# A two-layer hybrid decoder step: buffers for the S5 state tables, order of the first attention scores, and input projections by halves

## The chip, the cores and the metric

The kernel runs on one core of a Trainium2 chip. The metric is the device time of the program in microseconds, taken as the median of several executions. One further execution was recorded by the hardware profiler, and all trace times below are from it.

## The reference, cut to what matters

One inference step of two layers over 576 tokens: a prompt of 512 and 8 sequences of 8 new tokens each. Each layer has a token mixer with three branches on the same input and a channel mixer (dense SwiGLU in layer 0, top-2 of 8 experts in layer 1). Everything is fp32.

```python
def token_mixer(h, l, p, s5_re0, s5_im0, conv0, ssd0, past):
    gates, u, q, k, v, fg, z, xbc, dt_raw = jnp.split(h @ p['w_in'][l], _in_split_points(), axis=-1)
    gates = jax.nn.sigmoid(gates.reshape(bsz, seq, N_BRANCH, D_MODEL) + p['b_gate'][l])
    y_s5, s5_re, s5_im = s5_branch(u, s5_re0, s5_im0, ...)      # 32 groups of 16 channels, 64 complex states
    logf = jax.nn.log_sigmoid(fg + p['b_fgate'][l])
    y_fox = fox_prompt(q, k, v, logf) or fox_sample(...)        # 8 heads of 64, softmax with forget decay
    y_ssd, conv_new, ssd_new = ssd_branch(z, xbc, dt_raw, ...)  # y * silu(z), then an RMS norm
    merged = (gates[:, :, 0] * (y_s5 @ p['w_branch_s5'][l])
              + gates[:, :, 1] * (y_fox @ p['w_branch_fox'][l])
              + gates[:, :, 2] * (y_ssd @ p['w_branch_ssd'][l]))
    return merged @ p['w_o'][l], (k, v, logf, s5_re, s5_im, conv_new, ssd_new)

def run_trunk(x, p, ...):
    for l in range(2):
        x = layer_norm(ALPHA * x + token_mixer(x, l, ...), ln1_g[l], ln1_b[l])
        f = swiglu(x, ...) if l == 0 else moe_swiglu(x, ...)
        x = layer_norm(ALPHA * x + f, ln2_g[l], ln2_b[l])
```

The model width is 1024, each branch is 512 wide. The outputs are the tokens and all new states.

## The kernel before, in words

**Layout.** The input x lies transposed in SBUF, channels on 128 partitions and the 576 tokens along the free axis, as a high and a low part (`xh`, `xl`) whose sum is the fp32 value. A weight block of 128 output columns is loaded by SP (`wload`, L266, 512 KB), split into `wh` on ACT (L98) and `wl` on DVE (L107), and multiplied by `mm3` (L290 to L297): for each half of the tokens (288) and each of eight blocks of the contraction three matmuls, so 24 matmuls a half block and 48 a block. `colblocks` (L301) does this for several blocks in a row; with `by_half` it goes through all blocks for the first half of the tokens and then loads and splits the weights again for the second half.

**Order.** SP issues its DMAs in program order. The instructions of all other engines are ordered ahead of time by a planner, which simulates the engines and gives precedence by program order. `tc.issue_after(ins)` puts the instructions of its block behind `ins` on that instruction's engine. Tiles come from pools with a fixed number of buffers for each tag; a new tile waits until the tile that had the buffer before is no longer read. In the mixer's phases tag A has 7 buffers, T has 3, and K and Q have 1 each. PSUM has two buffers for `mm`, `px` and `pf` and one for `pa` and `p5`.

**Start.** Five tiles of x are loaded and transposed (`x_tr`), the first two blocks of the S5 projection u are loaded early, and `u_proj(0)` (L709) runs with hooks that put the transposes of x, the parameter DMAs (`params_dma`, 13 small ones, L693 and L695) and the steps of the S5 preparation (`s5_steps`, 14 small DMAs, L342 to L360) between its half blocks.

**Mixer** (L727). In both layers the forget gates (`fd`) come first, then the convolution state; then, in layer 1, `u_proj(1)`. In layer 0 u_proj ran at the start, and eight gate blocks stand in this place. Then come the convolution and SSD, keys, queries, values and attention (`kqv_fox`, L803), the S5 scan and its output loop, sampled attention, filler projections (gates and z that are needed later), the S5 gated unit and its product.

**Attention.** `kqv(j)` projects the K, Q and V blocks of two heads, transposes them and stores them to DRAM through ACT's queue; the last evictions are at L830. `kqv(0)` and `kqv(1)` come before the first head. For each of 8 heads and 4 blocks of queries, `front` loads kT and qT (POOL's queue), computes the scores (L886) and the softmax on DVE and ACT, and three units later `back` transposes the probabilities and multiplies by V (L909).

**S5 output loop** (L607 to L632). For each quarter q of the groups, ACT's queue loads `tu` (eight DMAs, tag T) and `cu`, the tables that carry the state (two DMAs, L613, tag A); eight pairs of matmuls for each of two halves add the products (L621 with tu, L622 with cu) into one PSUM tile (`p5`), which ACT evicts as `yg` before a GELU on DVE and ACT.

**Merge.** `mixer_end` (L1554) loads the attention output, calls `gate_z` (L1219), which multiplies the SSD output by the z gates and normalises it (squares on ACT summed on POOL, a matmul with ones at L1242, a square root, a reciprocal), and then `merge` (L1368): for eight column blocks the gated product of branch 1 (`front`), and, three blocks later, that of branch 2 (`back`), which alone needs the result of gate_z.

**End.** `combine` normalises five tiles of tokens and applies scale and shift with 1024 columns, 768 on DVE and 256 on POOL (L1913 to L1931).

Of the kernel before, what the change touches and what calls it, by code (L numbers as in the profile page):

```python
# [19 lines left out]
P = 128  # L20
D = 1024
# [13 lines left out]
NOV = -(-(576 - CAP) // CAP)  # L35
LT = (NOV + 1) * CAP
FLAG, SLAG, ZLAG = 3, 1, 1
CD_ = 768
NPRE, NPS, NPP = 5, 2, 1
LAGE = 1  # L40
NZ = (1, 1)
# [5 lines left out]
def decoder_step(ctx, tc, A, O):  # L47
# [251 lines left out]
    HS = (slice(0, HF), slice(HF, T))  # L299

    def colblocks(src, c0, ncol, kt, x, evac, by_half=False, first=()):  # L301
        first = list(first)
        for hs in (((0,), (1,)) if by_half else ((0, 1),)):
            for j in range(ncol // P):
                w = wsplit(first.pop(0) if first else wload(src, c0 + j * P, P, kt), P, kt)
                o = [MM()[:, :HF] for h in hs]
                mm3(o, w, kt, x, [HS[h] for h in hs])
                for h, o_ in zip(hs, o):
                    evac(j, h, o_)
# [198 lines left out]
    def s5_scan_and_out(l):  # L508
# [97 lines left out]
        for q in range(4):  # L606
            tus = U("T", [P, 8, P], name="tu")  # L607
            for s in range(8):
                act.dma_start(out=tus[s * 16:(s + 1) * 16],
                              in_=KZ[l][q, :, (1 + s) * 16:(1 + s) * 16 + P].rearrange("(g c) t -> c g t", c=16))  # L610
            cu = UA([P, 2, 4, 144], name="cu")
            for i in range(2):
                act.dma_start(out=cu[i * 64:i * 64 + 64],  # L613
                              in_=CD[l][:, i, q * 4:q * 4 + 4].rearrange("(a n) g t -> n a g t", a=2))
            for a in range(2):
                tu = tus[:, a:8:2]
                pt = P5()
                pv = pt[:, :288].rearrange("p (g k) -> p g k", g=4)
                for g in range(4):
                    gp = q * 4 + g  # L620
                    pe.matmul(pv[:, g, :], lhsT=tu[:, g, :], rhs=uc[a][:, gp, :], start=True, stop=False)  # L621
                    pe.matmul(pv[:, g, :], lhsT=cu[:, a, g, 16:144], rhs=vs[a][:, gp, 0:72], start=False, stop=True)  # L622
                yv = yg[a][:, q * 4:q * 4 + 4, :]
                y2v = [wk.tile([P, HF], F32, name="ygl", tag="v288", bufs=4).rearrange("p (g k) -> p g k", g=4)
                       for i in range(2)]
                cp(yv, pv)
                mul(dve, y2v[0], yv, yv)
                dve.tensor_scalar(y2v[0], y2v[0], 0.044715, 1.0, op0=OP.mult, op1=OP.add)
                mul(dve, y2v[0], y2v[0], yv)
                act.activation(y2v[1], y2v[0], AF.Tanh, scale=math.sqrt(2.0 / math.pi))  # L630
                stt(yv, y2v[1], 1.0, yv, OP.add, OP.mult)
# [94 lines left out]

    def mixer(l):  # L727
        w_in = A["w_in"][l]
        raw = wload_fd(w_in)
        w = wsplit(raw, 16, 8)  # L730
        fd = wk.tile([16, T], F32, name="fd", tag="xp", bufs=4)
# [45 lines left out]
        cp(cs8.rearrange("p a b -> p (a b)"), pt[:, :192])  # L777
        S["cs8"] = cs8

        if l:  # L780
            u_proj(l)
        else:
            for j in range(8):
                gate_out(l, 0, j)
                if j % 2:
                    with tc.issue_after(S["mm"].ins):
                        next(s5g)
                    next(s5g, None)
# [17 lines left out]
    def kqv_fox(l, w_in):  # L806
# [60 lines left out]
        def front(hp, i, h2):  # L867
            if i == 0 and h2 == 0:
                kqv_[hp] = U("V", [P, 512], name="vt")
                pool.dma_start(out=kqv_[hp], in_=VD[l][hp])  # L870
            h = 2 * hp + h2
            if i == 0:
                kq_[h] = kT, qT = U("K", [P, 2, 512], F32R, name="kT"), U("Q", [P, 512], F32R, name="qT")
                hd = slice(h2 * 64, h2 * 64 + 64)
                for a in range(2):
                    pr_ = slice(a * 64, a * 64 + 64)
                    pool.dma_start(out=kT.bitcast(F32)[pr_], in_=KD[l][hp][hd])
                    pool.dma_start(out=qT.bitcast(F32)[pr_], in_=QD[l][hp][hd, a])
                cb_[h] = U("CB", [P, 512], name="cb")
                pool.dma_start(out=cb_[h], in_=CTD[l][h].unsqueeze(0).to_broadcast([P, 512]))  # L880
            kT, qT = kq_[h]
            n = (i + 1) * P
            qs = slice(i * P, n)
            pt = PF()
            for a in range(2):
                pe.matmul(pt[:, :n], lhsT=qT[:, qs], rhs=kT[:, a, 0:n], start=(a == 0), stop=(a == 1))  # L886
            s_ = W5("s")
            stt(s_[:, :n], pt[:, :n], ct[:, i, h:h + 1], cb_[h][:, :n], OP.add, OP.subtract)
            sub(dve, s_[:, qs], s_[:, qs], pos)
            sm = wk.tile([P, 3], F32, name="smx", bufs=4)  # L890
            dve.tensor_reduce(sm[:, 0:1], s_[:, :n], axis=AX.X, op=OP.max, negate=True)
            act.activation(s_[:, :n], s_[:, :n], AF.Exp, bias=sm[:, 0:1], accum_out=sm[:, 1:2])
            dve.reciprocal(sm[:, 2:3], sm[:, 1:2])
            dve.tensor_scalar(s_[:, :n], s_[:, :n], sm[:, 2:3], None, op0=OP.mult)
            return s_
# [449 lines left out]
            pool.dma_start(out=t[2], in_=GD[l][j])  # L1345
            act.dma_start(out=MD[l][j], in_=gated(l, 0, j, yv, t)[2])

    def merge(l, yf, ys, mhl):
        seq = [(2, j) for j in range(8)] if 1 in SPILL[l] else \
            [(1, 0), (1, 1), (1, 2)] + [x for j in range(5) for x in ((1, j + 3), (2, j))] + [(2, 5), (2, 6), (2, 7)]  # L1350
        ready = {}
# [6 lines left out]
        def front(j):  # L1358
# [6 lines left out]
            else:  # L1365
                gates(GLEAD)
                t = ready.pop((1, j))
            t = gated(l, 1, j, yf, t)  # L1368
            for h in range(2):
                add(dve, m5[:, HS[h]], m5[:, HS[h]], t[h])  # L1370
            return m5

        def back(j, m5):
            gates(GLEAD)
            t = gated(l, 2, j, ys, ready.pop((2, j)))
            for h in range(2):
                add(dve, m5[:, HS[h]], m5[:, HS[h]], t[h])
                split(mhl[0][:, j, HS[h]], mhl[1][:, j, HS[h]], m5[:, HS[h]])
# [174 lines left out]

    def mixer_end(l, out, done=None):  # L1554
        yf = load_yf(l)
        ys = gate_z(l, A["w_in"][l])
        mhl = [V2([U("M", [P, 2, T], F32R, name=f"m{q}{i}") for i in range(4)]) for q in "hl"]
        merge(l, yf, ys, mhl)
        mixer_out(l, mhl, out, done)

    with phase("mix0", **MA):
# [5 lines left out]
        for i in range(3):  # L1567
            x_tr(i)
        gather_logs(0)
        s5g = s5_steps(0)  # L1570
        u_proj(0, (((0, 0), lambda: x_tr(3)), ((1, 0), lambda: x_tr(4)), ((1, 0), lambda: params_dma(0)),
                   ((2, 0), lambda: next(s5g)), ((0, 1), lambda: params_tr(0)), ((1, 1), lambda: next(s5g)), ((3, 1), lambda: next(s5g))), uw)
        mixer(0)
    with phase("mix0b", **MB):
        mixer_end(0, to_x)
# [335 lines left out]
    def combine(yy):  # L1911
# [3 lines left out]
        for i in range(5):  # L1915
# [5 lines left out]
            act.activation(ag[:n, 2:3], ag[:n, 1:2], AF.Sqrt, scale=ALPHA ** 2, bias=eps[:n, 0:1])  # L1921
            dve.reciprocal(ag[:n, 2:3], ag[:n, 2:3])
            stt(ag[:n, 3:4], ag[:n, 0:1], -1.0, ag[:n, 2:3], OP.mult, OP.mult)
            cc = (slice(0, CD_), slice(CD_, D))
            for en, cs in ((pool, cc[1]), (dve, cc[0])):
                act.activation(xt[:n, cs], xt[:n, cs], AF.Identity, scale=ag[:n, 2:3], bias=ag[:n, 3:4])
                mul(en, xt[:n, cs], xt[:n, cs], lb_[:n, 0, cs])
                add(en, xt[:n, cs], xt[:n, cs], lb_[:n, 1, cs])
            c0, c1 = cc
            o = O[0][0, i * P:(i + 1) * P] if i < 4 else O[1].rearrange("b t d -> (b t) d")  # L1930
            sp.dma_start(out=o, in_=xt[:n])  # L1931

# [83 lines left out]
```

## Time and profile before

| what | value |
|---|---|
| median of 3 runs | 2424.92 us (2424.42 to 2428.13) |
| profiled execution, its own time | 2409.88 us |
| its span | 2408.2 us |
| PE busy | 2284.0 us (95%) |
| DVE busy | 1578.5 us (66%) |
| ACT busy | 1142.8 us (47%) |
| POOL busy | 565.6 us (23%) |
| HBM traffic over the span | 166 GB/s |

The busy shares are averages over stages. PE is the engine with the least idle time, so a stage is read by two columns: PE's busy time in it, and the clock that PE was granted. Times in a trace are counted from the span's start.

### The profile page before, as it was taken

To read this page: it belongs to the slowest core of one execution; us is meant where nothing else is said; L and a number is where in the kernel's file an instruction comes from. 1 tells how busy PE (TensorE), PEld (TensorE's weight loads), DVE (VectorE), ACT (ScalarE), POOL (GpSimd) and SP (SyncE) were. 2 spreads that over 40 slices of the span, in tenths; PEclk is the share of its full clock that TensorE was granted. 3 is DMA by queue.
4 is the path that set the end of the run, shared out by engine and by line. 5 is a ranking of instruction groups with operands and counts; after the bars stand their busy time and mean duration, and the time that the engine had idled before them with its cause. 6 is when DMAs were issued, how large, how long until landed. Compare 5 with 4: busy or idle time off the path is not lost. (4 is left out here: it accounts for less than half of the span.)

```text
span 2408.2 us, 45404 instructions
## 1 busy us (share of the span) xinstructions
PE 2284.0 (95%) x17037; PEld 2161.2 (90%) x17038; DVE 1578.5 (66%) x3733; ACT 1142.8 (47%) x2551; POOL 565.6 (23%) x722
## 2 busy tenths in 40 slices
PE   7899999998999999999899999899999799999995
PEld 7898988778998999999799997789999599999995
DVE  7865678546588843334774587455547578888886
ACT  4354443453346323233554443353334477777773
POOL 8723223233130110001124323233003321110002
PEclk9999999999999999999999999899999899999998
DMA  7665558757445432233475656667234699999993
GB/s 191 180 186 164 158 151 203 186 149 224 118 126 156 147 98 80 80 88 106 126 198 161 177 150 179 168 176 217 81 98 123 179 252 258 254 256 255 238 249 97
DMA packets 588395, 402.26 MB, mean 167 GB/s; under 512 B 59372, under 2 KB 548124, under 8 KB 588136
## 3 DMA queue, kind: packets, MB, share of 16 engines
q1 hardware_dynamic: 479432, 238.39, 37.6%
q0 software_dynamic: 30912, 95.12, 14.3%
q10 hardware_dynamic: 77824, 65.78, 9.3%
q8 instruction: 136, 2.23, 0.4%
q14 instruction: 91, 0.75, 0.1%
HBM read 328.38 MB, written 70.92 MB: 166 GB/s over the span
## 5 line engine op out<-in xcount | busy, mean ns | idle before, releaser
L107 DVE TENSOR_TENSOR wl<-wr,wh 128x512 fp32r<-128x512 f32 x894 | 629.3, 713 | 370.6 <-ACT wh L98 350.7
L98 ACT ACTIVATE wh<-wr 128x512 fp32r<-128x512 f32 x894 | 554.1, 625 | 532.7 <-PE mm L296 394.6
L295 PE MATMUL mm<-xh,wh 128*128 128x288 f32 (+1 forms) x2048 | 619.8, 303 | 12.4 <-ACT wh L98 8.2
L297 PE MATMUL mm<-xh,wl 128*128 128x288 f32 (+1 forms) x2048 | 615.0, 300 | 2.0 <-DVE wl L107 2.0
L296 PE MATMUL mm<-xl,wh 128*128 128x288 f32 (+1 forms) x2048 | 614.7, 300 | 0.0
L295 PEld LDWEIGHTS mm<-xh,wh 128*128 128x128 f32 (+1 forms) x2048 | 387.7, 189 | 25.2 <-ACT wh L98 9.5
L297 PEld LDWEIGHTS mm<-xh,wl 128*128 128x128 f32 (+1 forms) x2048 | 387.0, 189 | 8.8 <-issue 3.3
L296 PEld LDWEIGHTS mm<-xl,wh 128*128 128x128 f32 (+1 forms) x2048 | 387.7, 189 | 6.9 <-issue 4.7
L1763 PE MATMUL pf<-xe,wh 128*128 128x352 f32 x448 | 131.2, 356 | 2.3 <-DVE eu L104 2.3
L1763 PE MATMUL mm<-xe,wh 128*128 128x352 f32 x448 | 133.4, 358 | 0.0
L1764 PE MATMUL mm<-xe,wl 128*128 128x176 f32 x512 | 117.6, 250 | 0.0
L1764 PE MATMUL pf<-xe,wl 128*128 128x176 f32 x512 | 117.5, 250 | 0.0
L295 PE MATMUL mm<-hq,wh 128*128 128x288 f32 x352 | 104.2, 296 | 0.2 <-DVE rf L104 0.2
L295 PE MATMUL pf<-xh,wh 128*128 128x288 f32 x352 | 104.3, 296 | 0.0
L297 PE MATMUL mm<-hq,wl 128*128 128x288 f32 x352 | 104.2, 296 | 0.0
L297 PE MATMUL pf<-xh,wl 128*128 128x288 f32 x352 | 104.1, 296 | 0.0
L296 PE MATMUL pf<-xl,wh 128*128 128x288 f32 x352 | 103.8, 295 | 0.0
L296 PE MATMUL mm<-hq,wh 128*128 128x288 f32 x352 | 103.7, 295 | 0.0
L1764 PEld LDWEIGHTS mm<-xe,wl 128*128 128x128 f32 x512 | 97.3, 193 | 0.0
L1764 PEld LDWEIGHTS pf<-xe,wl 128*128 128x128 f32 x512 | 97.0, 193 | 0.0
L1763 PEld LDWEIGHTS pf<-xe,wh 128*128 128x128 f32 x448 | 85.4, 191 | 2.6 <-DVE eu L104 2.6
L1763 PEld LDWEIGHTS mm<-xe,wh 128*128 128x128 f32 x448 | 86.2, 192 | 0.0
(664 smaller groups left out, 5290.4 us busy)
## 6 DMA issues: line engine op xcount, KB each, us to landing
wr<-in_w_in_dram SPq DMA_DIRECT2D x112, 512.0 KB
wr<-in_moe_w_gate_dram SPq DMA_DIRECT2D x64, 512.0 KB
wr<-in_moe_w_up_dram SPq DMA_DIRECT2D x64, 512.0 KB
wr<-in_moe_w_down_dram SPq DMA_DIRECT2D x64, 512.0 KB
wr<-in_w_o_dram SPq DMA_DIRECT2D x32, 512.0 KB
wr<-in_ffn_w_gate_dram SPq DMA_DIRECT2D x25, 512.0 KB
wr<-in_ffn_w_up_dram SPq DMA_DIRECT2D x25, 512.0 KB
wr<-in_ffn_w_down_dram SPq DMA_DIRECT2D x24, 448.0 KB
```

What stands on the lines that cost most here:

```text
L98: return act.activation(out, in_, AF.Copy)
L107: e.tensor_tensor(out, a, b, op=OP.subtract)
L295: pe.matmul(o, lhsT=wh_[:, a, :m], rhs=x[0][:, k, s], start=(st and k == 0), stop=False)
L296: pe.matmul(o, lhsT=wh_[:, a, :m], rhs=x[1][:, k, s], start=False, stop=False)
L297: S["mm"] = pe.matmul(o, lhsT=wl_[:, a, :m], rhs=x[0][:, k, s], start=False, stop=(sp_ and k == kt - 1))
L1763: pe.matmul(o, lhsT=h_[:, k % 4, :], rhs=xf, start=(k == 0), stop=False)
L1764: pe.matmul(o[:, 0:CAP], lhsT=l_[:, k % 4, :], rhs=x[:, k, 0], start=False, stop=False, skip_group_check=True)
```

## The change: what it does

Six edits.

1. `colblocks` has a path of its own for weights that were loaded early (`first`): each is split once, and all of them are used for the first half of the tokens and then for the second; the other blocks are loaded once and used for both halves. Only `u_proj(0)` passes such weights (u0 and u1). Its hooks are placed anew: `x_tr(3)` behind u0's first half, `x_tr(4)` behind u1's first half, the S5 DMAs behind u0's second half, the parameter DMAs behind u1's second half, the next S5 step behind u2, and the rest behind u3. `u_proj(1)` passes none and keeps the loop by halves.
2. In the S5 output loop the table `cu` of odd quarters lies in a T tile and holds only the 128 columns that are read (four DMAs in place of two); even quarters keep the A tile.
3. `u_proj(1)` goes from behind the convolution state to the front of `mixer(1)`.
4. The four scores of head 0 are put behind the last matmul issued through `mm3` at that place, the last of V1 in `kqv(1)`.
5. `gate_z` is called inside `merge`, behind the gated product of the first block of branch 1, and its instructions on PE stand behind that product's last matmul.
6. `combine` no longer splits the columns: one ACT step and two DVE steps of 1024 columns for each tile, none on POOL.

```diff
--- before.py
+++ after.py
@@ -35,7 +35,6 @@
 NOV = -(-(576 - CAP) // CAP)
 LT = (NOV + 1) * CAP
 FLAG, SLAG, ZLAG = 3, 1, 1
-CD_ = 768
 NPRE, NPS, NPP = 5, 2, 1
 LAGE = 1
 NZ = (1, 1)
@@ -299,10 +298,23 @@
     HS = (slice(0, HF), slice(HF, T))
 
     def colblocks(src, c0, ncol, kt, x, evac, by_half=False, first=()):
-        first = list(first)
+        if first:
+            ws = [wsplit(raw, P, kt) for raw in first]
+            for h in range(2):
+                for j, w in enumerate(ws):
+                    o = MM()[:, :HF]
+                    mm3([o], w, kt, x, [HS[h]])
+                    evac(j, h, o)
+            for j in range(len(ws), ncol // P):
+                w = wsplit(wload(src, c0 + j * P, P, kt), P, kt)
+                o = [MM()[:, :HF] for h in range(2)]
+                mm3(o, w, kt, x, HS)
+                for h in range(2):
+                    evac(j, h, o[h])
+            return
         for hs in (((0,), (1,)) if by_half else ((0, 1),)):
             for j in range(ncol // P):
-                w = wsplit(first.pop(0) if first else wload(src, c0 + j * P, P, kt), P, kt)
+                w = wsplit(wload(src, c0 + j * P, P, kt), P, kt)
                 o = [MM()[:, :HF] for h in hs]
                 mm3(o, w, kt, x, [HS[h] for h in hs])
                 for h, o_ in zip(hs, o):
@@ -608,10 +620,18 @@
             for s in range(8):
                 act.dma_start(out=tus[s * 16:(s + 1) * 16],
                               in_=KZ[l][q, :, (1 + s) * 16:(1 + s) * 16 + P].rearrange("(g c) t -> c g t", c=16))
-            cu = UA([P, 2, 4, 144], name="cu")
-            for i in range(2):
-                act.dma_start(out=cu[i * 64:i * 64 + 64],
-                              in_=CD[l][:, i, q * 4:q * 4 + 4].rearrange("(a n) g t -> n a g t", a=2))
+            if q % 2:
+                cu = U("T", [P, 8, P], name="cu").rearrange("p (a g) t -> p a g t", a=2)
+                for i in range(2):
+                    for a in range(2):
+                        act.dma_start(out=cu[i * 64:i * 64 + 64, a],
+                                      in_=CD[l][a * 64:a * 64 + 64, i, q * 4:q * 4 + 4, 16:144])
+            else:
+                cu = UA([P, 2, 4, 144], name="cu")
+                for i in range(2):
+                    act.dma_start(out=cu[i * 64:i * 64 + 64],
+                                  in_=CD[l][:, i, q * 4:q * 4 + 4].rearrange("(a n) g t -> n a g t", a=2))
+                cu = cu[:, :, :, 16:144]
             for a in range(2):
                 tu = tus[:, a:8:2]
                 pt = P5()
@@ -619,7 +639,7 @@
                 for g in range(4):
                     gp = q * 4 + g
                     pe.matmul(pv[:, g, :], lhsT=tu[:, g, :], rhs=uc[a][:, gp, :], start=True, stop=False)
-                    pe.matmul(pv[:, g, :], lhsT=cu[:, a, g, 16:144], rhs=vs[a][:, gp, 0:72], start=False, stop=True)
+                    pe.matmul(pv[:, g, :], lhsT=cu[:, a, g], rhs=vs[a][:, gp, 0:72], start=False, stop=True)
                 yv = yg[a][:, q * 4:q * 4 + 4, :]
                 y2v = [wk.tile([P, HF], F32, name="ygl", tag="v288", bufs=4).rearrange("p (g k) -> p g k", g=4)
                        for i in range(2)]
@@ -726,6 +746,8 @@
 
     def mixer(l):
         w_in = A["w_in"][l]
+        if l:
+            u_proj(l)
         raw = wload_fd(w_in)
         w = wsplit(raw, 16, 8)
         fd = wk.tile([16, T], F32, name="fd", tag="xp", bufs=4)
@@ -777,9 +799,7 @@
         cp(cs8.rearrange("p a b -> p (a b)"), pt[:, :192])
         S["cs8"] = cs8
 
-        if l:
-            u_proj(l)
-        else:
+        if l == 0:
             for j in range(8):
                 gate_out(l, 0, j)
                 if j % 2:
@@ -882,8 +902,9 @@
             n = (i + 1) * P
             qs = slice(i * P, n)
             pt = PF()
-            for a in range(2):
-                pe.matmul(pt[:, :n], lhsT=qT[:, qs], rhs=kT[:, a, 0:n], start=(a == 0), stop=(a == 1))
+            with tc.issue_after(S["mm"].ins) if h == 0 else nullcontext():
+                for a in range(2):
+                    pe.matmul(pt[:, :n], lhsT=qT[:, qs], rhs=kT[:, a, 0:n], start=(a == 0), stop=(a == 1))
             s_ = W5("s")
             stt(s_[:, :n], pt[:, :n], ct[:, i, h:h + 1], cb_[h][:, :n], OP.add, OP.subtract)
             sub(dve, s_[:, qs], s_[:, qs], pos)
@@ -1345,7 +1366,8 @@
             pool.dma_start(out=t[2], in_=GD[l][j])
             act.dma_start(out=MD[l][j], in_=gated(l, 0, j, yv, t)[2])
 
-    def merge(l, yf, ys, mhl):
+    def merge(l, yf, mhl):
+        ys = []
         seq = [(2, j) for j in range(8)] if 1 in SPILL[l] else \
             [(1, 0), (1, 1), (1, 2)] + [x for j in range(5) for x in ((1, j + 3), (2, j))] + [(2, 5), (2, 6), (2, 7)]
         ready = {}
@@ -1366,13 +1388,16 @@
                 gates(GLEAD)
                 t = ready.pop((1, j))
             t = gated(l, 1, j, yf, t)
+            if j == 0:
+                with tc.issue_after(S["mm"].ins):
+                    ys.append(gate_z(l, A["w_in"][l]))
             for h in range(2):
                 add(dve, m5[:, HS[h]], m5[:, HS[h]], t[h])
             return m5
 
         def back(j, m5):
             gates(GLEAD)
-            t = gated(l, 2, j, ys, ready.pop((2, j)))
+            t = gated(l, 2, j, ys[0], ready.pop((2, j)))
             for h in range(2):
                 add(dve, m5[:, HS[h]], m5[:, HS[h]], t[h])
                 split(mhl[0][:, j, HS[h]], mhl[1][:, j, HS[h]], m5[:, HS[h]])
@@ -1553,9 +1578,8 @@
 
     def mixer_end(l, out, done=None):
         yf = load_yf(l)
-        ys = gate_z(l, A["w_in"][l])
         mhl = [V2([U("M", [P, 2, T], F32R, name=f"m{q}{i}") for i in range(4)]) for q in "hl"]
-        merge(l, yf, ys, mhl)
+        merge(l, yf, mhl)
         mixer_out(l, mhl, out, done)
 
     with phase("mix0", **MA):
@@ -1568,8 +1592,9 @@
             x_tr(i)
         gather_logs(0)
         s5g = s5_steps(0)
-        u_proj(0, (((0, 0), lambda: x_tr(3)), ((1, 0), lambda: x_tr(4)), ((1, 0), lambda: params_dma(0)),
-                   ((2, 0), lambda: next(s5g)), ((0, 1), lambda: params_tr(0)), ((1, 1), lambda: next(s5g)), ((3, 1), lambda: next(s5g))), uw)
+        u_proj(0, (((0, 0), lambda: x_tr(3)), ((1, 0), lambda: x_tr(4)), ((0, 1), lambda: next(s5g)),
+                   ((1, 1), lambda: params_dma(0)), ((2, 1), lambda: next(s5g)), ((3, 1), lambda: params_tr(0)),
+                   ((3, 1), lambda: next(s5g))), uw)
         mixer(0)
     with phase("mix0b", **MB):
         mixer_end(0, to_x)
@@ -1921,12 +1946,9 @@
             act.activation(ag[:n, 2:3], ag[:n, 1:2], AF.Sqrt, scale=ALPHA ** 2, bias=eps[:n, 0:1])
             dve.reciprocal(ag[:n, 2:3], ag[:n, 2:3])
             stt(ag[:n, 3:4], ag[:n, 0:1], -1.0, ag[:n, 2:3], OP.mult, OP.mult)
-            cc = (slice(0, CD_), slice(CD_, D))
-            for en, cs in ((pool, cc[1]), (dve, cc[0])):
-                act.activation(xt[:n, cs], xt[:n, cs], AF.Identity, scale=ag[:n, 2:3], bias=ag[:n, 3:4])
-                mul(en, xt[:n, cs], xt[:n, cs], lb_[:n, 0, cs])
-                add(en, xt[:n, cs], xt[:n, cs], lb_[:n, 1, cs])
-            c0, c1 = cc
+            act.activation(xt[:n], xt[:n], AF.Identity, scale=ag[:n, 2:3], bias=ag[:n, 3:4])
+            mul(dve, xt[:n], xt[:n], lb_[:n, 0])
+            add(dve, xt[:n], xt[:n], lb_[:n, 1])
             o = O[0][0, i * P:(i + 1) * P] if i < 4 else O[1].rearrange("b t d -> (b t) d")
             sp.dma_start(out=o, in_=xt[:n])
 
```

## Rows read from the trace of the kernel before

**Rows 1.** The page's busy line: engine, busy us (share of the span) x instructions.

```profile
PE 2284.0 (95%) x17037; PEld 2161.2 (90%) x17038; DVE 1578.5 (66%) x3733; ACT 1142.8 (47%) x2551; POOL 565.6 (23%) x722
```

**Rows 2.** Windows: length, busy of each engine (x instructions), PEclk, DMA share, GB/s.

```profile
0.00:60.00 60.00, 45.92 (x305) 41.96 (x307) 45.60 (x194) 24.93 (x57) 49.04 (x72) 0.91 0.77 191
195.00:220.00 25.00, 19.01 (x146) 18.24 (x145) 11.13 (x20) 8.41 (x22) 8.33 (x11) 0.86 0.66 192
405.00:505.00 100.00, 88.79 (x733) 74.80 (x736) 50.65 (x124) 45.45 (x116) 35.03 (x51) 0.95 0.75 189
505.00:560.00 55.00, 54.74 (x509) 50.72 (x502) 28.49 (x62) 21.13 (x45) 13.02 (x20) 1.00 0.63 184
560.00:600.00 40.00, 33.34 (x223) 31.82 (x222) 29.18 (x51) 18.59 (x37) 18.47 (x32) 0.87 0.66 211
900.00:960.00 60.00, 60.00 (x455) 60.00 (x454) 19.91 (x36) 18.51 (x37) 0.00 (x0) 1.00 0.30 86
1160.00:1230.00 70.00, 63.17 (x418) 57.59 (x417) 48.49 (x132) 37.23 (x87) 8.83 (x19) 0.93 0.60 151
1300.00:1325.00 25.00, 21.70 (x164) 21.00 (x162) 8.31 (x16) 8.34 (x17) 10.76 (x12) 0.93 0.47 141
1490.00:1545.00 55.00, 43.31 (x247) 36.43 (x247) 22.20 (x59) 15.89 (x41) 11.12 (x17) 0.78 0.68 166
1655.00:1700.00 45.00, 43.12 (x288) 42.15 (x287) 27.97 (x51) 24.50 (x44) 17.17 (x26) 0.89 0.52 162
```

**Rows 3.** Waits of PE: us in total, times, longest.

```profile
PE pf L886 <- DMA qT<-QD: 8.7, 2, 5.4
PE mm L295 <- DVE gt L110: 3.6, 1, 3.6
PE px L1242 <- POOL lns L104: 3.0, 1, 3.0
```

**Rows 4.** Timeline of SP and PE at the start: start us, us, engine, operation.

```profile
19.09 0.43 SPq L266 DMA_DIRECT2D wr<-in_w_in_dram  x1
28.71 2.29 SPq L266 DMA_DIRECT2D wr<-in_w_in_dram  x3
33.66 0.61 PE L295 MATMUL mm<-xh,wh 128*128 128x288 f32 x1 [2.86 <-ACT wh L98]
```

**Rows 5.** Timeline of PE and ACT around attention's first scores and its end.

```profile
213.28 1.19 PE L886 MATMUL pf<-kT,qT 128*128 128x128 f32 x4 [5.42 <-DMA qT<-QD]
235.66 1.06 PE L886 MATMUL pf<-kT,qT 128*128 128x384 f32 x4
246.60 0.40 ACT L830 ACTIVATE kq<-mm 128x288 f32<-128x288 f32 x1
487.58 0.65 PE L233 MATMUL px<-ident,kpg 128*128 128x128 f32 x4 [2.05 <-ACT yfs L98]
492.19 0.98 PE L909 MATMUL pf<-pT,vt 128*64 128x128 f32 x7
1306.29 0.30 PE L886 MATMUL pf<-kT,qT 128*128 128x128 f32 x1 [3.30 <-DMA qT<-QD]
1332.83 1.05 PE L886 MATMUL pf<-kT,qT 128*128 128x384 f32 x4
```

**Rows 6.** Timeline of ACT's queue and PE in the S5 output loop.

```profile
423.65 1.29 ACTq L613 DMA_DIRECT2D cu<-CD  x2
433.28 0.41 PE L622 MATMUL p<-V,cu 128*128 128x72 f32 x2 [4.16 <-DMA cu<-CD]
1521.75 0.68 PE L622 MATMUL p<-V,cu 128*128 128x72 f32 x2 [3.56 <-DMA FD<-yo]
```

**Rows 7.** Timeline of PE at layer 1's start.

```profile
1183.51 0.66 PE L295 MATMUL mm<-xh,wh 128*16 128x288 f32 x2 [4.21 <-ACT xh L98]
```

**Rows 8.** DVE lines by form, 2389 to 2405: busy us, mean ns.

```profile
L104 DVE TENSOR_TENSOR cx<-cx,lnb 128x768 f32<-128x768 f32 x4 | 5.7, 1444 | 0.0
L104 DVE TENSOR_TENSOR cx<-cx,lnb 64x768 f32<-64x768 f32 x1 | 0.9, 941 | 0.0
```

## The prediction, made before the change was built or run

> **What bounds the kernel now.** I read the busy line first: TensorE (PE) is busy for 2284.0 us of a span of 2408.2, and no other engine comes near [rows 1]. So the time is PE's work plus what PE loses, and nearly all of the diff touches the loss. PE loses in two ways, and the windows show both [rows 2]. One is idle time, a window's length less its PE column. The other is work at the lower of two clock levels, 1.2 instead of 2.4 GHz: the granted clock (the column after the engines) falls below 1.00 in every window in which PE stood still, and is 1.00 in 505 to 560 and 900 to 960, where it did not. In 900 to 960 455 matmuls run without a gap, 0.132 us each; a half block of 24 is 3.15 us. I price the clock as (1 - granted) x length, which takes all of the lost clock as lost work, an upper end. Then the places that the diff touches lose, idle + clock:
>
> - start, 0 to 60: 14.1 + 5.4
> - first attention scores, 195 to 220 and 1300 to 1325: 6.0 + 3.5 and 3.3 + 1.8
> - S5 output loop, 405 to 505 and 1490 to 1545: 11.2 + 5.0 and 11.7 + 12.1
> - z gates and merge, 560 to 600 and 1655 to 1700: 6.7 + 5.2 and 1.9 + 5.0
> - layer 1's start, 1160 to 1230: 6.8 + 4.9
>
> That is 61.7 idle and 42.9 clock, at most 104.6 us that edits here can reach. The waits view names which release ended the idle time [rows 3], and timelines of PE, ACT and SP show what stood behind each.
>
> **The change part by part**, against the profiled execution.
>
> *S5 input projection, layer 0.* Each of the eight half blocks loaded its own weights. Now u0 and u1 are split once for both halves, and u2 and u3 are loaded once: 4 loads of 512 KB and 8 pairs of splits fewer. But SP issues in program order, and u2's load, which went out at 19.09 behind 13 parameter DMAs and ahead of 14 S5 DMAs, now stands behind all 27, so it leaves at about 28.7, where u3's left before [rows 4]. There PE waited 2.86 us and restarted at 33.66 [rows 4] with three half blocks done; now it restarts at the same time with four done, since both halves of u0 and u1 need no new weights. Gain one half block, 3.2 us. Below: u2 and u3 now both come late and the wait repeats, 0. Above: the four loads saved (2 MB at 191 GB/s in that window [rows 2], 10 us of transfer) bring every later weight forward, 6. I take 3.2.
>
> *First scores queued behind projections.* In each layer PE came to head 0's first score and waited for the load of qT: 5.42 us in layer 0 [rows 5], both layers 8.7 [rows 3]. The change puts the four scores of head 0 behind the last matmul of the projections' last block (V1), so PE runs projections while qT lands. The wait goes, with its clock: of the two windows' 9.3 + 5.3 I take 8.7 and 4.5, gain 13.2. In return head 0 starts later. V1's eviction ends at 247.0 in layer 0 [rows 5], while the score of block 2 ran at 235.66: the attention chain starts some 11 us later there, and about 2 in layer 1, where V1's last matmul ends near 1335 and the like score stood at 1332.83 [rows 5]. That chain (scores, softmax on DVE and ACT, P times V, one K and one Q buffer) runs until 492.19, 279 us for 32 units of head and block, 8.7 each, and PE runs out of other work at its end (2.05 us at 487.58) [rows 5]. Where other blocks are still at hand when it ends the delay costs nothing: 505 to 560 holds 54.74 us of PE work in 55 [rows 2], though some of it needs S5's result. So 0 to 13; I take 8 lost.
>
> *Carried-state tables in two buffers.* Each of four quarters loads cu, and its buffer was free only after the last matmul of the quarter before. In layer 0 the loads leave at 423.65 and PE waits until 433.28, 4.16 of it idle; in layer 1 it waits 3.56 until 1521.75 [rows 6] (the profile names a store; the matmul wants cu too). Odd quarters now use the T tiles (three buffers, shared with tu), so quarter q+1 loads while q computes. ACT's queue holds four odd loads for two, 2 x 2 more issues of some 0.65 us each in a layer [rows 6], before tu's of the next quarter; ACT has slack there (45.45 of 100 [rows 2]). The two waits shown are 7.7 us, and like ones of the later quarters bring it to 10 of the 22.9 idle in the two windows [rows 2]; of 17 us of clock in the two windows I give 4 to them. Gain 14. Below 0: T's three buffers now carry tu and cu, so a tu may wait for a cu where it didn't. Above, all that the loop loses with its clock: 22.
>
> *z gates inside the merge.* gate_z needs a norm whose POOL and DVE steps stood ahead of the first gated product: PE waited 2.95 us for lns and 3.62 for gt [rows 3]. Behind the first gated block, the norm's chain has that block's PE time (12 matmuls a half, about 3 us) as cover, and DVE reaches gt first. Of 6.7 + 5.2 and 1.9 + 5.0 I take 4: the first gt still needs its own gate, and the norm's chain is as long as before, so the second wait can move to the second block. Between 0 and 16.
>
> *S5 input projection, layer 1, moved to the front.* PE waited 4.21 us for xh, the normalised input, at 1183.51, and the window is 70 us with 418 matmuls, 55 us of them at 0.132 [rows 2, 7]. The first matmul there belongs to the forget gates' second half, and the projection's half 0, whose input is ready, stood behind it. Now that half (four half blocks, 12.6 us) goes first and covers the wait, its clock and the later waits for the convolution state. Of 6.8 + 4.9 I take 10; between 2 (the weights for it come late) and 11.7.
>
> *Tail without POOL.* Five tiles are scaled and shifted; before, 768 columns on DVE and 256 on POOL. A DVE operation took 1444 ns beside POOL and 941 in the last tile, of 64 partitions, with POOL nearly done [rows 8]. At 1444 per 768 the ten of 1024 would take 19.3 us, a loss of 5.4 on the 13.9 that they take now (nine near 1.444, one 0.941); at 941 per 768 they take 12.5, a gain of 1.4, less something for the ACT step of 1024 columns that now comes before the first. I take 1, by the row without POOL. The Trainium skill ("SBUF — State Buffer", section "Who interferes with whom") says that a tensor_tensor with both inputs in SBUF contends with GpSimd's reads, by which the 1444 is POOL's doing and not 128 partitions'; by that rule this end stands and the loss of 5.4 falls away.
>
> Sum: 3.2 + 13.2 - 8 + 14 + 4 + 10 + 1 = 37.4, so an execution like the profiled one (2409.88) takes 2372.5. The median of the runs is 2424.92, 15.0 above it; I carry this over: 2387.5, and forecast **2387**.
>
> **The rivals.**
>
> *Waits only move.* PE's order is planned, and one order changed in six places can bring new waits and new low-clock stretches. For: V1's block ends late, and the windows show how a wait of 3 us is followed by as much again at the low clock. Against: the waits removed have named causes that go. The start, the move of layer 1 and a part of the loop remain, 3 + 10 + 5: time 2407.
>
> *Everything closes.* The chain's delay is hidden, and S5 and merge lose nothing: 6 + 13 + 22 + 10 + 11 + 1 = 63: time 2362. For: PE has filler work (505 to 560). Against: PE was already short of work at 487.58 [rows 5].
>
> *Slower: attention is the bound.* Place: from V1 to the last P times V. If its 279 us don't shrink, and now begin only after V1 for all of head 0 (26 us behind the softmax of blocks 0 and 1 in layer 0: 213.28 + 8.7 against 247; about 24 in layer 1, whose first score stood at 1306.29 [rows 5]), PE has nothing to put beside the last heads, and the gains at the scores and the S5 loop fall within its wait. It decides from where the delay is more than the fillers left, some 55 us less what S5 holds back. Price: 50 - (3.2 + 4 + 10 + 1) - some 17 that fillers still cover = 15 slower: time 2440. For: 32 units at 8.7 us each in a row. Against: PE is full until 405, so the chain is paced by PE's share as well, and can catch up.
>
> *It does nothing.* The planner puts the same instructions in the same places apart from the tail and the start: 2421. Against: the diff pins the order.
>
> **How the numbers follow.** Forecast 48%, own range 2375 to 2402 (chain 13 or 0 for 8, gates 0 to 12, loop 6 to 20). Waits move 24%, all closes 14%, slower 9%, nothing 5%. The range over the cases: 2360 to 2418. A change under 0.2% (4.8 us) can't be told from none here. Faster: 48 + 24 + 14 = 86%; same 6%, half of them from the case of nothing; slower 8%.
>
> **What would show it.** PE's busy time hardly moves (2284 less a part of the lost clock, 2265 to 2285), and the span falls. The wait for qT is gone or under 1 us; if the last P times V falls after 500 the chain's delay is real. The waits at the cu matmuls fall under 1 us each; if tu appears as their releaser, the shared buffers took the wait over. 1160 to 1230 shows no idle time over 1 us. PE restarts after the start's weights at about 33, not later. DVE operations in the tail near 1.2 us; near 1.9 I am wrong there. The forecast is wrong if span less PE busy, now 124.2 us [rows 1], stays above 108.

## The result, and the profile after

The changed kernel takes **2401.06 us** (2399.84 to 2405.59, 4 runs) beside 2426.27 for the kernel before (2424.42 to 2428.13), a ratio of 0.9888 (0.9861 to 0.9916). Two more comparisons gave 0.9874 (0.9851 to 0.9896) and 0.9903 (0.9877 to 0.993).

One thing has to be taken out first. From 20 to 40 us nearly nothing runs in the first profile of the changed kernel, and nothing of the kind is in the first profile of the kernel before. The window from 20 to 40, columns as in [rows 2], in the kernel before, profiled a second time (e1), then in the changed kernel's first profile, then in its third (e9):

```profile
20.00:40.00 20.00, 3.33 (x13) 2.23 (x11) 2.28 (x12) 0.93 (x2) 15.14 (x16) 0.65 0.53 110
```
```profile
20.00:40.00 20.00, 3.85 (x14) 2.59 (x12) 0.00 (x0) 0.00 (x0) 12.37 (x13) 0.61 0.30 62
```
```profile
20.00:40.00 20.00, 18.75 (x135) 18.46 (x134) 13.26 (x88) 8.10 (x24) 15.84 (x17) 0.91 0.58 127
```

PE runs 13 or 14 matmuls where it runs 135. Timelines of SP and PE in the changed kernel's first profile show how:

```profile
22.57 0.73 SPq L713 DMA_DIRECT2D prow<-in_ln_g_dram  x1
24.00 0.70 SPq L713 DMA_DIRECT2D prow<-in_ln_b_dram  x1
24.70 0.72 SPq L713 DMA_DIRECT2D prow<-in_ln_g_dram  x1
26.12 0.70 SPq L713 DMA_DIRECT2D prow<-in_ln_b_dram  x1
```
```profile
24.73 0.40 PE L295 MATMUL mm<-xl,wh 128*128 128x288 f32 x1 [1.84 <-issue]
26.86 0.40 PE L296 MATMUL mm<-xh,wl 128*128 128x288 f32 x1 [1.73 <-issue]
```

SP's and PE's instructions come in steps of 0.70 us, and PE waits for nothing but "issue". I call it the crawl. It stands in five of the first six profiles (not in the first of the kernel before) and in none of the eight later ones, whichever kernel ran. Beside the profiles that have it the kernel before took 2426 to 2428 us, beside the eight later ones 2401 to 2408. So stages are compared between the two profiles without it: [rows 1 to 8] for before, and e9 for the changed kernel. The busy line of e9 (span 2381.4, own time 2383.01):

```profile
PE 2278.5 (96%) x17037; PEld 2158.7 (91%) x17038; DVE 1574.1 (66%) x3725; ACT 1133.9 (48%) x2538; POOL 560.6 (24%) x712
```

Span less PE busy is 102.9 us for 124.2, under the 108 that the prediction set as its limit; in the changed kernel's first profile, with the crawl, it is 121.3. The windows of e9 that answer to [rows 2]:

```profile
0.00:60.00 60.00, 50.56 (x347) 47.47 (x349) 47.37 (x217) 23.26 (x52) 49.40 (x68) 0.94 0.71 176
225.00:250.00 25.00, 25.00 (x197) 23.90 (x196) 17.70 (x43) 12.97 (x33) 7.70 (x10) 1.00 0.57 164
390.00:490.00 100.00, 90.47 (x645) 75.85 (x645) 54.17 (x139) 41.92 (x109) 29.16 (x40) 0.86 0.71 177
575.00:615.00 40.00, 32.58 (x218) 31.06 (x217) 28.63 (x56) 15.96 (x31) 9.87 (x17) 0.87 0.41 117
1150.00:1225.00 75.00, 70.50 (x484) 65.58 (x483) 48.80 (x122) 43.35 (x98) 6.18 (x11) 0.95 0.64 164
1310.00:1330.00 20.00, 20.00 (x159) 19.30 (x157) 14.98 (x31) 9.80 (x23) 10.81 (x13) 1.00 0.69 193
1498.00:1545.00 47.00, 38.85 (x230) 34.24 (x228) 22.30 (x60) 17.23 (x47) 9.24 (x14) 0.75 0.68 161
```

Read the second and sixth against the third and seventh. Where the first scores stood, PE is now fully busy at the full clock. But layer 0's S5 stretch, 390 to 490, lost 11.2 us idle and 5.0 of clock before and now loses 9.5 and 14, and layer 1's still loses 8.2 and 11.8. The waits at the scores are gone, but the S5 stretch is worse in layer 0 (23.5 us lost for 16.2) and little better in layer 1 (20.0 for 23.8). The merge (575 to 615) idles 7.4 for 6.7.

Lengths of the stages, each from the first matmul that begins it to the first of the next (us; e1, the kernel before again, is given for the crawl):

| stage | before | e1 | changed (e9) | e6 no scores | e7 no second buffer | e11 neither | e12 scores behind K1 |
|---|---|---|---|---|---|---|---|
| start, to the SSD sums | 178.2 | 197.9 | 169.9 | 168.6 | 168.4 | 168.9 | 168.8 |
| layer 0 attention and S5 | 399.2 | 394.8 | 397.7 | 386.4 | 393.9 | 396.0 | 395.3 |
| layer 0 merge | 93.9 | 93.9 | 94.9 | 94.1 | 93.8 | 95.2 | 93.8 |
| output projection, FFN | 488.6 | 488.6 | 488.4 | 487.8 | 487.8 | 488.3 | 487.9 |
| layer 1 start | 110.1 | 116.8 | 105.8 | 105.6 | 105.0 | 105.5 | 105.7 |
| layer 1 attention and S5 | 401.7 | 402.8 | 398.0 | 385.6 | 394.2 | 387.6 | 382.6 |
| layer 1 merge | 143.4 | 140.3 | 139.1 | 143.2 | 139.6 | 139.6 | 140.0 |
| rest | 593.1 | 591.5 | 587.8 | 583.6 | 590.2 | 589.9 | 592.6 |

The last five columns differ in the rest by up to 9 us, although their edits do not touch it, so a few us of one stage in one profile prove little.

### The profile page after: what moved, and what is told of

The parts are those of the page before. It is cut to its first block, busy times and chain, and to the rows that moved or that the text cites. A ratio compares the mean times of both kernels' runs of the same rounds, so it can differ in the third digit from the quotient of the medians.

```text
span 2398.7 us, 45369 instructions
## 1 busy us (share of the span) xinstructions
PE 2277.4 (95%) x17037; PEld 2158.2 (90%) x17038; DVE 1573.7 (66%) x3725; ACT 1134.5 (47%) x2538; POOL 560.4 (23%) x712
## 5 line engine op out<-in xcount | busy, mean ns | idle before, releaser
L1337 ACT ACTIVATE gt<-mm,prm 128x288 f32<-128x288 f32 x96 | 47.4, 494 | 85.4 <-PE mm L296 75.1
```

What stands on the lines that cost most here:

```text
L1337: act.activation(t[h], o[h], AF.Tanh, scale=0.5, bias=prm[l][:, c0:c0 + 1])
```

## The experiments

Each is the kernel named with the edit shown. Medians stand beside the kernel before on the same chip; ratios are to it.

**e1 and e2: both kernels again.** No edit.

> The kernel before, unchanged, for a second profile of it. Theory A (stalls in which no engine gets its instructions, as PE, ACT, DVE and SP show it in the changed kernel's profile from 20 to 40 us, come and go from one execution to the next and are not tied to the new order): an execution near 2424 us shows such a stall of some 15 us somewhere, at the start or near 1920, which the first profile (2409.88) did not have. Theory B (the stall belongs to the new order of the start): no stall from 20 to 40, PE restarts at 33.7 as in the first profile, and the time is again near 2410.

> The changed kernel, unchanged, for a second profile. Theory A: the stall from 20 to 40 us is elsewhere, shorter or gone, and an execution without it takes some 2380 to 2388. Theory B: the stall stands at the same place with the same 20 us, and the time is 2400.

e1 took 2428.11 with the crawl; e2 2397.33 (before: 2428.11), ratio 0.9874, with the crawl at the same place. The crawl is not tied to the new order, since the kernel before has it. It lengthens the start of the kernel before by 19.7 us and that of the changed kernel by 16 (185.7 and 186.6 for 169.9). Theory B fell. Theory A is right that the order is not the cause; that an execution of the changed kernel without the crawl takes some 2380 to 2388 was seen only in e9 (2383.01).

**e3 and e4: the start alone.** e3 is the changed kernel with `colblocks` and the hooks as before, e4 the kernel before with them as in the change.

```diff
-        if first:
-            ws = [wsplit(raw, P, kt) for raw in first]
...
+        first = list(first)
...
-        u_proj(0, (((0, 0), lambda: x_tr(3)), ((1, 0), lambda: x_tr(4)), ((0, 1), lambda: next(s5g)),
+        u_proj(0, (((0, 0), lambda: x_tr(3)), ((1, 0), lambda: x_tr(4)), ((1, 0), lambda: params_dma(0)),
...
```

> The changed kernel with the start as before (colblocks without its path for early weights, hooks as before). By the forecast's term the start is worth 3.2 us, so 3 us slower than the changed kernel (2404). Theory A: within 4 us of that. Theory B: the stall is gone, layer 0's projection ends near 52 and not 65 us, and the time is 13 to 16 us less than the changed kernel's, near 2386.

> The kernel before with the new start alone. By the forecast's term 3 us faster than before (2422). Theory A: the same within 4 us. Theory B: 10 to 13 us slower than before, with the stall from 20 to 40 us in its trace.

e3: 2411.91, ratio 0.9932 (0.9905 to 0.9959), 14.6 us above e2. e4: 2418.08, ratio 0.9964 (0.9942 to 0.9987), 10 us below before. Both keep the crawl. All the numbers expected missed: beside the crawl the new start is worth 9 to 15 us by the medians, and 11 to 12 by the stage (197.9 in e1 and 198.0 in e3, for 185.7 and 186.6 in the changed kernel and 186.4 in e4).

**e5: the gathers later.** The changed kernel with the indirect gathers of the cached log-forget values put behind.

```diff
-        gather_logs(0)
         s5g = s5_steps(0)
...
+        with tc.issue_after(S["late"].ins):
+            gather_logs(0)
         mixer(0)
```

> The changed kernel with the 16 indirect gathers of the cached log-forget values (POOL, from 7 us on) put behind the store of the projection's first block. Theory G (the crawl of PE and SP from 20 to 40 us, one instruction every 0.70 us, comes of the gathers that run beside it and ends some 4 us after they pause): PE and SP issue at their normal pace from 20 to 40, PE waits only for u2's weights near 33, and the time falls by 10 to 16 us below the changed kernel's, to some 2382 to 2388; it may return for a few us where the gathers now stand. Rival (the crawl has to do with the start of the program, not with the gathers): it stands from 20 to 40 as before, time within 4 us of the changed kernel's 2398.

2378.03 (before: 2407.98), ratio 0.987 (0.9843 to 0.9898): no gain beyond the interval. No crawl stands in its profile, but none in those of e6, e7 and e8 either, which ran beside it with their gathers from 7 us on. Theory G lost its ground: gathers beside the start do not bring the crawl by themselves.

**e6: no order for the scores.** The changed kernel without it.

```diff
-            with tc.issue_after(S["mm"].ins) if h == 0 else nullcontext():
-                for a in range(2):
-                    pe.matmul(pt[:, :n], lhsT=qT[:, qs], rhs=kT[:, a, 0:n], ...)
+            for a in range(2):
+                pe.matmul(pt[:, :n], lhsT=qT[:, qs], rhs=kT[:, a, 0:n], ...)
```

> The changed kernel without the order of head 0's scores. By the forecast's term (13.2 gained at the wait for qT, 8 lost by the attention chain's delay) 5 us slower than the changed kernel: 2403, with the waits for qT of 5.4 and 3.3 us back and the last P times V some 10 us earlier. Rival (the delayed chain costs nothing, since PE has other work until it ends): 10 to 13 us slower, 2409. Second rival (waits only move: PE waits elsewhere as long): within 3 us.

**2361.03, ratio 0.9811 (0.9785 to 0.9837)**: 0.0077 below the mean of the changed kernel's three ratios and 0.0092 below that of e9, so by the ratios to the kernel before 18 to 22 us faster than the changed kernel (some 10 to 30 by the intervals), against all three expectations. With the second buffer in place the order costs; without it the kernel beats both. Its waits for qT are 3.76 us in layer 0 and none in layer 1.

**e7: one buffer for the tables.** The changed kernel with every `cu` in the A tile.

```diff
-            if q % 2:
-                cu = U("T", [P, 8, P], name="cu").rearrange("p (a g) t -> p a g t", a=2)
-                ...
-            else:
-                ...
+            cu = UA([P, 2, 4, 144], name="cu")
...
+                    pe.matmul(pv[:, g, :], lhsT=cu[:, a, g, 16:144], rhs=vs[a][:, gp, 0:72], ...)
```

> The changed kernel with all state tables in the A tile again. By the forecast's term 14 us slower: 2412, with waits for cu of 3 to 4 us in both layers' loops. Rival (the loop's waits only move to tu and to the table's next load, as the changed kernel's waits of 2.8 us for tu at 435 and 5.2 us for cu at 1536 have it): within 5 us.

2377.84, ratio 0.9879 (0.9849 to 0.9909): the same as the changed kernel. In this order the second buffer is worth nothing.

**e8: layer 1's projection late.** The changed kernel with `u_proj(1)` behind the convolution state.

```diff
-        if l:
-            u_proj(l)
         raw = wload_fd(w_in)
...
+        if l:
+            u_proj(l)
+        else:
```

> The changed kernel with layer 1's input projection behind the convolution state again. By the forecast's term 10 us slower: 2408, with the wait of 4.2 us for xh at the forget gates' second half back. Rival (the wait moves with the half that comes second: 1.9 and 2.3 us for xh and xl remain in the changed kernel near 1187): 4 to 5 us slower, 2402.

2383.22, ratio 0.9894 (0.986 to 0.9928). The stage of layer 1's start takes 110.7 us for 105.8, so 4.9, as the rival has it; the medians cannot tell it from nothing.

**e9: the changed kernel a third time**, as the base of e10 to e12.

> The changed kernel, unchanged, beside the three that follow, as their base. Without the crawl from 20 to 40 us some 2375 to 2380 where the kernel before takes 2408 (ratio 0.986 to 0.989); with it 2397 to 2401 at 2428, the same ratio.

2379.43 (before: 2401.28), without the crawl; the ratio, 0.9903 (0.9877 to 0.993), is just above the range expected.

**e10: z gates before the merge.** The changed kernel with gate_z called in mixer_end.

```diff
+        ys = gate_z(l, A["w_in"][l])
         mhl = ...
...
-            if j == 0:
-                with tc.issue_after(S["mm"].ins):
-                    ys.append(gate_z(l, A["w_in"][l]))
```

> The changed kernel with gate_z before the merge again. By the forecast's term 4 us slower than the changed kernel. Rival (the waits for lns and gt only stand one block later: 4.1 and 2.9 us in the changed kernel for 3.0 and 3.6 before): within 3 us, and the stage from the first gated product to the output projection lasts 94 us in layer 0 and 139 to 143 in layer 1, as in the changed kernel.

2372.95, ratio 0.9879 (0.9847 to 0.9912). The merges take 93.6 and 139.0 us, for 94.9 and 139.1: the rival holds, the edit gains nothing.

**e11: neither scores nor second buffer** (both edits, of e6 and e7).

> The changed kernel without the order of the scores and with all state tables in the A tile. Theory (the second buffer is worth its 14 us or more, but only where the attention chain leaves PE fillers for the S5 loop, and the scores' order takes these away): 14 to 22 us slower than the kernel without the scores' order alone (ratio 0.9811), so about 0.988 of the kernel before. Rival (the second buffer is worth nothing in either order): ratio 0.980 to 0.983.

2373.74, ratio 0.9884 (0.9855 to 0.9913), against 0.9811 with the second buffer (e6): 0.0073, 17.5 us, with the intervals some 8 to 27. So once the scores are free the second buffer is worth its forecast of 14. Of the 16.0 us between the two profiles 9.6 lie in layer 0's stage with the S5 loop and only 2.0 in layer 1's; 6.3 lie in the rest, which the edit does not touch. And with one buffer the order of the scores costs nothing: 0.9879 (e7) beside 0.9884.

**e12: scores behind K1.** The changed kernel with the four scores behind an earlier block.

```diff
                 o = dense(w_in, c0 + j * P, 8, X)
+                if c0 == C_K:
+                    S["k"] = S["mm"]
...
-            with tc.issue_after(S["mm"].ins) if h == 0 else nullcontext():
+            with tc.issue_after(S["k"].ins) if h == 0 else nullcontext():
```

> The changed kernel with head 0's scores behind the last matmul of K1 instead of V1, two blocks (12.6 us of PE) earlier. Theory (the cost of the order is the delay of the attention chain, 15 us in layer 1 and some 24 in layer 0): in layer 1 no delay is left and in layer 0 about half, so most of the 14 us come back: ratio 0.981 to 0.984. Rival (it is the pinned order and not its place that costs): 0.987 to 0.989, as with V1.

2366.33, ratio 0.9848 (0.9819 to 0.9877), just past the theory's end and short of the rival's. The stages tell more. Layer 1, where the first score now stands at 1298.9, 47 us into its stage (e6: 49, the changed kernel: 60), has the whole gain, 382.6 us. Layer 0, where it stands 44 us into the stage (e6: 37, the changed kernel: 59), keeps most of the cost, 395.3, which the place of the first score alone doesn't explain; there the last P times V still stands 326 us into the stage (e6: 306, the changed kernel: 331), while in layer 1 it stands at 302 (309 and 318). So the place costs, not the pin, in layer 1; for layer 0 this stays open.

## Why the prediction came out as it did

**The sum came near by errors that in part offset each other.** The direction is right, but 2401 lies at the edge of the forecast's own range (2402) and nearer to the rival in which waits only move (2407) than to 2387, and two parts below, gate_z and layer 1's start, show that rival's mechanism. Between profiles without the crawl the gain is 26.8 us (2408.2 to 2381.4) for 37.4. By stages: start 8.3 (forecast 3.2), scores and tables together 1.5 + 3.7 = 5.2 (13.2 - 8 + 14 = 19.2), layer 1's start 4.3 (10), merges 3.3 (4, none of it gate_z's by e10), the end of the kernel 5.3 of which the tail, from PE's last matmul on, is some 2 (1; 22.4 to 20.2). That start and end gained more than forecast is luck for the sum: it hides a part of the 14 us that are missing at scores and tables.

**The step that failed is the cover for the attention chain's delay**: "So 0 to 13; I take 8 lost." e6 puts the order's whole effect, beside the second buffer, at 18 to 22 us lost where 5.2 gained was forecast, so the delay cost more than the wait that it removed, and the slower rival had the direction at the scores, though in layer 1 PE did not run out of work, as it has it (below). The forecast took the delay at block 2's score, 11 and 2 us; the rival took it at the first score, 26 (25 by its own rows) and 24, and that is what came: in e9 the first score stands 59.5 and 60.3 us into its stage, for 35.0 and 36.2 before, 24 later in each layer. The last P times V, whose place was the sign of a real delay, stands 331 us into layer 0's stage for 315 before, but 318 for 319 in layer 1.

**And the two terms do not add.** The ratios make a square:

| ratio to the kernel before | scores free | scores behind V1 |
|---|---|---|
| one buffer | 0.9884 (e11) | 0.9879 (e7) |
| second buffer | 0.9811 (e6) | 0.9888, 0.9874, 0.9903 (changed) |

Either edit spoils the other: the second buffer gains only with the scores free, and the order costs only beside the second buffer. Together they are worth nothing against neither, where the sum has 13.2 - 8 + 14 = 19.2. By the stages, one profile each, the order costs layer 1 6.6 us even with one buffer (394.2 for 387.6), and layer 0 then gains 2.1.

Where the order's loss sits in layer 1, PE and ACT's queue show in the S5 loop. Windows over the loop, the changed kernel (e9) and e6:

```profile
1481.00:1540.00 59.00, 50.85 (x314) 44.08 (x313) 29.28 (x79) 18.78 (x51) 11.49 (x18) 0.80 0.66 164
```
```profile
1467.00:1515.00 48.00, 48.00 (x378) 42.48 (x377) 29.66 (x76) 19.37 (x52) 13.75 (x20) 1.00 0.88 214
```

The loop takes 48 us without a gap in e6, and 58 with 8 idle and the clock at 0.80 in e9. The last quarter's `cu` and its matmul in e9, then in e6:

```profile
1520.64 0.63 ACTq L627 DMA_DIRECT2D cu<-CD  x1
...
1524.71 0.58 ACTq L627 DMA_DIRECT2D cu<-CD  x1
1529.32 0.68 PE L642 MATMUL p<-V,cu 128*128 128x72 f32 x2 [4.74 <-DMA cu<-CD]
```
```profile
1498.46 0.63 ACTq L627 DMA_DIRECT2D cu<-CD  x1
1500.13 1.25 ACTq L627 DMA_DIRECT2D cu<-CD  x2
1508.66 0.39 PE L642 MATMUL p<-V,cu 128*128 128x72 f32 x2
```

In e9 the issues of the four loads are spread over 4 us, the last of them 4.6 before the matmul that then waited for it; in e6 they are out 8 us ahead, and meanwhile PE runs a filler, a projection block that nothing in the loop needs. The third block of layer 1's z projections starts at 1500.9 in e6, inside the loop, and at 1542.4 in e9, behind it. PE had not run out of fillers in e9. Its last projection matmul before the gap and the first behind it, and ACT's evictions of the two half blocks that were done by then, in e9, then the same two evictions in e6:

```profile
1500.46 0.29 PE L296 MATMUL mm<-xh,wl 128*128 128x288 f32 x1
...
1533.50 0.61 PE L294 MATMUL mm<-xh,wh 128*128 128x288 f32 x1
```
```profile
1526.31 0.42 ACT L1344 ACTIVATE zt__18755<-mm 128x288 f32<-128x288 f32 x1
1526.60 0.43 ACT L1344 ACTIVATE zt__18819<-mm 128x288 f32<-128x288 f32 x1
```
```profile
1491.45 0.43 ACT L1343 ACTIVATE zt__18755<-mm 128x288 f32<-128x288 f32 x1
1491.74 0.45 ACT L1343 ACTIVATE zt__18819<-mm 128x288 f32<-128x288 f32 x1
```

The tag `mm` has two buffers in PSUM, and in e9 both stay full from 1500.5 until ACT comes to them 26 us later, though ACT is busy for only 8.6 of these 25.8 us; in that stretch PE's clock is 0.74. So two things stand late on ACT in e9, the loads of `cu` and these evictions, and the second stops every projection. In layer 1 the longest gap without a projection matmul is 33 to 37 us in e9, e10 and the changed kernel's first two profiles, 26 in e7, and 11 in e6, e11 and e12. It is 30 in the kernel before, and e8 breaks the pattern, with 8 and a stage of 398.0, so the gap is not the whole of it.

This bears on layer 1's 12.4 us between e9 and e6, not on what the second buffer is worth, of which layer 1 has only 2.0 (e11 to e6). That loads and evictions stand late because the delayed attention units hold ACT's queue is my reading; the dose (e12) fits it in layer 1, and no run moved the loads or the evictions alone. Of layer 0 I can say only that e9 takes 397.7 for 386.4 in e6, and that its S5 stretch lost the clock, not the idle time. Even this is not the order's alone: the changed kernel's first two profiles, behind the crawl, take 389.1 and 389.3 in that stage, and e5, with the same order of the scores, 382.9.

**The start was under its size, and one detail was wrong.** "Now it restarts at the same time": PE doesn't stop for these weights at all. The 27 small DMAs went out by 25.55 in e9, and u2's load behind them at 25.59, where before u3's left at 28.71 [rows 4]; PE's only wait over 1 us between 20 and 60 is 1.25:

```profile
25.59 0.43 SPq L265 DMA_DIRECT2D wr<-in_w_in_dram  x1
```
```profile
24.98 0.28 PE L232 MATMUL px<-ident,prow 104*128 104x104 f32 x1 [1.25 <-DMA prow<-in_ssd_norm_w_dram]
```

So the wait of 2.86 went with its clock, and the start, to the SSD sums, gains 8.3.

**The two buffers** were right in mechanism: in e6 no wait for `cu` is left in either layer. In e9 two are left, both in layer 1 (2.12 and 4.74 us), where the prediction's sign was under 1. The condition was missed, that the loads leave early.

**gate_z** kept its chain, as feared, and gained nothing. PE, merge of layer 0, in e9:

```profile
582.67 0.85 PE L1263 MATMUL px<-lns,br 128*128 128x288 f32 x1 [4.47 <-POOL lns L103]
586.89 0.61 PE L294 MATMUL mm<-yfh,wh 128*128 128x288 f32 x1 [2.89 <-DVE gt L109]
```

7.4 us, for 6.6 [rows 3]: the waits stand one block later. Layer 1's merge fell from 143.4 to 139.1, but e10, without the edit, has 139.0 and e6, with it, 143.2: what moves it is open.

**u_proj(1)** gained half. The wait for xh [rows 7] did not go, it split, because the projection's second half needs the same input:

```profile
1180.42 0.53 PE L294 MATMUL mm<-xh,wh 128*128 128x288 f32 x2 [1.88 <-ACT xh L97]
1183.22 0.61 PE L295 MATMUL mm<-xl,wh 128*128 128x288 f32 x1 [2.28 <-DVE xl L106]
```

PE's idle time in that stage, summed, is 4.5 us in e9, 7.8 in e8 and 7.0 before; the forecast of 10 counted the wait as gone.

**The tail** went by the row without POOL. DVE, last 21 us of e9, lines by form:

```profile
L100 DVE TENSOR_TENSOR cx<-cx,lnb 128x1024 f32<-128x1024 f32 x4 | 4.8, 1218 | 0.8 <-ACT cx L1949 0.8
L103 DVE TENSOR_TENSOR cx<-cx,lnb 128x1024 f32<-128x1024 f32 x4 | 4.8, 1212 | 0.0
L103 DVE TENSOR_TENSOR cx<-cx,lnb 64x1024 f32<-64x1024 f32 x1 | 1.2, 1206 | 0.0
```

1024 columns take 1212 ns for 128 partitions and 1206 for 64, less than the 1444 that 768 took beside POOL [rows 8]. The rule of the Trainium skill ("SBUF — State Buffer", "Who interferes with whom"), that a tensor_tensor with both inputs in SBUF contends with GpSimd's reads, agrees with these rows.

**The 15.0 us carried over** from the first profile to the median were, as far as e1 shows (2428.11, its start 19.7 us longer than in that profile), the crawl, which the changed kernel has too. Carrying them did little harm: of the 14 us that part 2387 from 2401, 10.6 are the sum's (37.4 for 26.8).

## What to carry to other kernels

A chain of other engines can start behind a wait on the bottleneck engine; to move work in front of it saves the wait and starts the chain later, so ask where the chain ends and what must leave its queues by then. Gains that were worked out one by one need not add: here two edits together were worth nothing, and one of them alone 17.5 us, so run each pair that shares a queue or a stage without one of its halves. A second buffer can be worth nothing where its load leaves late: look at the issue time, not only at the buffer count. When the bottleneck engine idles although it has work, see who still holds its output buffers. Before a difference of 1% is read from one profile, look whether a second profile of the same kernel has the same stages.

## What had not been expected of the hardware

The crawl: for some 20 us near the start PE and SP took an instruction every 0.70 us or a multiple of it, with half the DMA traffic (62 GB/s for 127 in the windows above), while POOL kept its pace of one gather in 1.26 us. The kernel before has a span 18.3 us longer with it (2426.5 in e1 for 2408.2). Shorter waits for "issue", of up to 1.2 us each, stand near 1920 to 1950 in the same profiles. Its cause stays open: neither the order of the start (e1) nor the gathers by themselves (e6 to e8) bring it, and e1 to e4, which have it, ran on the same chip as e5 to e8, which do not.
